# Down products with side jobs: the next half's first low half tied behind the first addition, and the jobs behind the additions written so far

## The chip, the cores and the metric

The kernel runs on one core of a Trainium2 chip. The metric is the device time of one execution in microseconds (us), as the median of several runs. The engines are named as in the profile: PE is the tensor engine's matmuls and PEld its weight loads, DVE the vector engine, ACT the scalar engine, POOL the GpSimd engine, SP the engine whose queue issues most loads. L524 is line 524 of the kernel before.

## What is computed

A trunk of four layers over 512 positions of width 1024, in float32. Each layer has a mixer (two S5 layers, one gated linear attention, one differential attention) and then a feed-forward product:

```python
def swiglu_ffn(h, w_gate_up, w_down):
    g, u = jnp.split(h @ w_gate_up, 2, axis=-1)
    return (jax.nn.silu(g) * u) @ w_down
...
    for layer in range(DEPTH):
        kind = layer % N_MIXERS
        ...
        x = x + mix.astype(x.dtype)
        h = rmsnorm(x, norm_ffn[layer])
        x = x + swiglu_ffn(h, ffn_w_gate_up[layer], ffn_w_down[layer]).astype(x.dtype)
```

`w_gate_up` is 1024 by 5632 and `w_down` 2816 by 1024. The change lies in the down product, `(...) @ w_down`, of layers 0 and 1.

## The kernel before

**Products in three matmuls.** Each float32 operand is split into a high half in the format that PE multiplies quickly and a low half, the rest. A product of two 128-wide tiles is three matmuls, high by high, high by low and low by high (`mm3`, L396 to L398). A block of weights, 256 rows by 512 columns, goes through four steps: a load of 512 KB into a staging buffer (`staged`, tile `wst`, 3 buffers), a cast on ACT that makes the high half (`high`, L368, tile `whl`, 5 buffers), a subtraction on DVE that makes the low half (`low`, L376), and 24 matmuls (2 k-tiles by 4 row tiles by 3). A staging buffer is free again when its low half is made.

**The feed-forward stage.** `ffn` works through the hidden width in groups of blocks of 256: groups of 3, 3, 3 and 2 blocks in layer 0, and of 4, 4 and 3 in the others. For each group it makes the gate and up products (`seven_block`, seven block products each, L541), which leaves the activations in `act`, and then calls `gemm_b` twice, once for each 512 columns of the output (d = 0 and d = 1, the two halves), which multiplies the group's activations by its rows of `w_down`. A half accumulates in four PSUM banks, one for each 128 positions (t = 0 to 3). In the last k-tile each finished bank is added into x on DVE, scaled by a column r (L524, in `add_x`), which also frees the bank: the next half's products for tile t need it. In the last group each addition is followed by the next layer's norm for that tile (`left.take`: a multiplication on DVE, L107, then transposes on PE and a split of the result). The last group's second half has a tail: its last four k-tiles run tile by tile instead (in layer 0, where the last group has four k-tiles, that is the whole half).

**Side jobs.** Layers 0 and 1 use their down products to prepare operands for later mixers. A generator (`s5_spilled` in layer 0; `diff_tables` and then `s5_phases_spilled` in layer 1) is stepped once behind each tile's three matmuls (`self.job()`), and each step writes a few small instructions: on DVE (L1129 to L1131 and L1246 in layer 0, L1306 to L1312 in layer 1), on ACT, small matmuls on PE, and DMAs in POOL's queue. In layer 0 a round of the generator has 17 steps, with work in steps 1, 3, 5, 7, 9, 11 and 13 to 16, eight rounds in all; in layer 1 it is 13 steps of tables and then eight rounds of 14, of which the first eight do work.

**Order.** Within these stages the order of each engine's instructions is not written by hand. A planner that runs when the kernel is built keeps a modelled clock, and gives each engine the earliest-written instruction that is ready on it; the engines then run their queues in that order. `issue_after(ins)` adds an edge of order alone: what its block writes on the engine of `ins` is queued behind `ins`, with no wait. `job` uses it with every entry of `self.last`, the latest instruction of each of several kinds (high, low, scaled, silu, mm and others). `gemm_b` with jobs writes the split of the next weight block ahead of the current block's matmuls (`nxt`). In a first half, the later blocks' splits are tied behind the last gate's `silu` and `scaled` (`behind`).

Of the kernel before, what the change touches and what calls it, by code (L numbers as in the profile page):

```python
# [16 lines left out]
ALU = mybir.AluOpType  # L17
# [22 lines left out]
class Slices:  # L40


    def __init__(self, *tiles):
        self.ts, self.known = [[self.flat(t), 0] for t in tiles], {}
# [116 lines left out]
class Sides(Left):  # L161
# [27 lines left out]
    def ahead(self, n):  # L189

        w = [self.tr.staged(self.quarter(0, 0, b), 4, 256) for b in range(len(self.heads), len(self.heads) + n)]
        self.heads += [self.tr.halves(y, 4, 256) for y in w]
# [96 lines left out]
class Trunk:  # L289
    def __init__(self, ctx, tc, ins, out):  # L290
        self.ctx, self.tc, self.nc = ctx, tc, tc.nc
        self.i = ins
        self.out = out
        self.rot = self.edges = 0
        nc = self.nc
        ep = lambda name, bufs, **k: ctx.enter_context(tc.tile_pool(name=name, bufs=bufs, **k))
        self.cp = ep("const", 1)
        self.xp = ep("xp", 1)
        self.hp = ep("hp", 2)
        self.wp = ep("wp", 3)  # L300
        self.np_ = ep("normp", 2)
        self.sp = ep("small", 8)
        self.ps = ep("psum", 1, space=PSUM)
        self.dp = ep("dram", 1, space=DRAM)
        self.ident = self.cp.tile([P, P], F32, name="ident")
        make_identity(nc, self.ident)
        self.two_pi = float(np.nextafter(np.float32(TWO_PI), np.float32(0)))
        self.mhalf = self.cp.tile([P, 8], F32, name="mhalf")
        nc.vector.memset(self.mhalf[:], -0.5)
        self.ones = self.cp.tile([P, P], F32, name="ones")  # L310
        nc.gpsimd.memset(self.ones[:], 1.0)
        self.dq = nc.sync
        self.jobs = iter(())
        self.last = {}
        self.pend = []
        self.guard, self.lazy = None, False
        self.behind = None

    def edge(self, pool, n):

# [79 lines left out]
    def gemm_b(self, stat, w, nk, c0, evac, k0=0, tail=0, between=(), ahead=None, jobs=False, behind=None):  # L400

        between = iter(between)
        accs = [self.acc() for _ in range(NT)]
        hl = nxt = None
        for kb in range(0, nk - tail, 2):
            hl = nxt or self.wb(w, k0 + kb, c0)
            self.behind = behind
            nxt = self.wb(w, k0 + kb + 2, c0) if jobs and kb + 2 < nk - tail else None  # L410
            if kb == 2:
                self.flush()
            for a in range(2):
                k = kb + a
                for t in range(NT):
                    self.mm3(
                        accs[t][:], stat(k, 0, t), stat(k, 1, t), hl[:, 0, a], hl[:, 1, a],
                        k == 0, k == nk - 1,
                    )
                    if k == nk - 1:  # L420
                        evac(t, accs[t])
                    if jobs:
                        self.job()
            next(between, lambda: None)()
        self.behind = None
        if tail:
            hls = [self.wb(w, k0 + kb, c0) for kb in range(nk - tail, nk, 2)]
            if ahead:
                self.hand_all()
                ahead()  # L430
            for t in range(NT):
                for j in range(tail):
                    k = nk - tail + j
                    self.mm3(
                        accs[t][:], stat(k, 0, t), stat(k, 1, t), hls[j // 2][:, 0, j % 2],
                        hls[j // 2][:, 1, j % 2], k == 0, k == nk - 1,
                    )
                evac(t, accs[t])
# [76 lines left out]
    def add_x(self, d, left=None, r=None):  # L515

        nc = self.nc

        def evac(t, ps):
            xs = self.x[:, t, d * 512 : (d + 1) * 512]  # L520
            if r is None:
                nc.vector.tensor_tensor(xs, xs, ps[:], op=ALU.add)
            else:
                nc.vector.scalar_tensor_tensor(xs, ps[:], r[:, t : t + 1], xs, op0=ALU.mult, op1=ALU.add)  # L524
            if left is not None:
                left.take(t, d)

        return evac
# [2035 lines left out]
```

## Time and profile before

| what | value |
|---|---|
| time, median of 3 runs | 2266.39 us (2264.08 to 2268.05) |
| time of the profiled execution | 2265.08 us |
| span of the profiled execution | 2263.3 us |
| PE busy | 2200.7 us, 97% of the span |
| PEld busy | 1952.7 us, 86% |
| DVE busy | 1561.8 us, 69% |
| ACT busy | 1121.4 us, 50% |
| POOL busy | 281.2 us, 12% |
| additions into x, L524 | 96, median 0.75 us each |
| low halves, L376 | median 1.22 us each |

How to read it: a row of a timeline has the start and the duration in us, the engine, the line, the operation, the tiles written and read, the shape and the count, and in brackets how long the engine was idle before it and what it waited for. Instructions on DVE overlap a little: the next starts up to 0.09 us before the recorded end. The profiled execution's sums are made against its own 2265.08 us.

### The profile page before, as it was taken

The page shows a single profiled execution, that of the slowest core. Times are in us where ns is not written, and L with a number is a line of the kernel's source. Part 1 is how long each engine was busy: PE and PEld are TensorE (multiplying, and loading weights), DVE is VectorE, ACT ScalarE, POOL GpSimd, SP SyncE. Part 2 cuts the span into 40 slices and gives each one's busy share as a digit, 9 for nine tenths or more (in the row PEclk, how much of TensorE's full clock was granted, in tenths as well). Part 3 has the DMA queues.
Part 4 walks back from the last instruction along what each step waited for, and adds up shares of the span by engine and source line. Part 5 has one row for each costly group of instructions (what it writes and reads, how often), then busy time and mean ns, then how long its engine had stood idle before and what let it go on. Part 6 is the DMA issues. An engine that isn't in the chain of part 4 may idle for free.

```text
span 2263.3 us, 37243 instructions
## 1 busy us (share of the span) xinstructions
PE 2200.7 (97%) x14847; PEld 1952.7 (86%) x14847; DVE 1561.8 (69%) x2424; ACT 1121.4 (50%) x1878; POOL 281.2 (12%) x392
## 2 busy tenths in 40 slices
PE   5999999999999999999999999999999899999998
PEld 4878979889777799998988887999998788989997
DVE  9963977776625479777754675977766964967675
ACT  6534645453453456555535676744544224635343
POOL 1000141522000011101002131111000100101000
PEclk8999999999999999999999999999999999999999
DMA  4257475663422557766336366985641546676632
GB/s 88 52 154 188 115 192 159 172 188 90 124 75 65 142 143 185 191 162 172 99 127 142 91 147 161 237 219 134 175 101 39 147 144 166 169 186 158 168 75 75
DMA packets 296039, 317.83 MB, mean 140 GB/s; under 512 B 72285, under 2 KB 235417, under 8 KB 295482
## 3 DMA queue, kind: packets, MB, share of 16 engines
q1 hardware_dynamic: 233626, 234.23, 34.4%
q0 software_dynamic: 62240, 81.22, 19.3%
q8 instruction: 117, 1.92, 0.4%
q14 instruction: 56, 0.46, 0.1%
HBM read 283.54 MB, written 16.65 MB: 133 GB/s over the span
## 4 chain that ended last, share of the span: by engine, by line
PE 83%; DVE 8%; ACT 4%; issue 2%; DMA 1%; SPq 1%; POOL 0%; ACTq 0%; DVEq 0%; POOLq 0%
PE a L541 18%; PE acc L396 14%; PE acc L398 13%; PE acc L397 13%; PE c L541 8%; PE d L541 4%; PE y L1504 2%; DVE whl L376 2%; ACT whl L368 1%; PE V L1468 1%; PE op L2366 1%; PE s L2332 1%; PE tp L123 1%; DVE halves L229 1%; ACT halves L211 1%
## 5 line engine op out<-in xcount | busy, mean ns | idle before, releaser
L376 DVE TENSOR_TENSOR whl<-wst,whl 128x1024 fp32r<-128x1024 f32 x272 | 331.2, 1222 | 260.7 <-ACT whl L368 260.2
L368 ACT CAST whl<-wst 128x1024 fp32r<-128x1024 f32 x272 | 283.9, 1050 | 310.3 <-PE acc L398 227.2
L541 PE MATMUL a<-side,whl 128*128 128x256 f32 x3168 | 382.3, 277 | 4.0 <-DVE whl L376 3.6
L541 PEld LDWEIGHTS a<-side,whl 128*128 128x128 f32 x3168 | 369.0, 188 | 6.8 <-DVE whl L376 5.4
L396 PE MATMUL acc<-whl,act 128*128 128x512 f32 x680 | 268.9, 396 | 1.9 <-DVE x L524 1.9
L397 PE MATMUL acc<-whl,act 128*128 128x512 f32 x680 | 265.3, 390 | 0.0
L398 PE MATMUL acc<-whl,act 128*128 128x512 f32 x680 | 265.3, 390 | 0.0
L541 PE MATMUL c<-side,whl 128*128 128x256 f32 x2112 | 254.3, 277 | 1.2 <-DVE whl L376 1.2
L541 PEld LDWEIGHTS c<-side,whl 128*128 128x128 f32 x2112 | 246.7, 188 | 2.0 <-DVE whl L376 2.0
L376 DVE TENSOR_TENSOR whl<-slot,whl 128x1024 fp32r<-128x1024 f32 x107 | 130.4, 1221 | 70.4 <-ACT whl L368 70.4
L396 PEld LDWEIGHTS acc<-whl,act 128*128 128x128 f32 x680 | 127.6, 188 | 31.3 <-issue 2.7
L368 ACT CAST whl<-slot 128x1024 fp32r<-128x1024 f32 x107 | 112.2, 1053 | 83.0 <-PE acc L398 34.9
L398 PEld LDWEIGHTS acc<-whl,act 128*128 128x128 f32 x680 | 127.7, 188 | 27.0
L397 PEld LDWEIGHTS acc<-whl,act 128*128 128x128 f32 x680 | 127.7, 188 | 24.7
L396 PE MATMUL acc<-whl,hT 128*128 128x512 f32 x352 | 142.6, 405 | 0.0
L398 PE MATMUL acc<-whl,hT 128*128 128x512 f32 x352 | 138.1, 392 | 0.0
L397 PE MATMUL acc<-whl,hT 128*128 128x512 f32 x352 | 137.8, 392 | 0.0
L541 PE MATMUL a<-sides,whl 128*128 128x256 f32 x1056 | 134.5, 283 | 0.0
L541 PEld LDWEIGHTS a<-sides,whl 128*128 128x128 f32 x1056 | 129.7, 191 | 1.2
L541 PE MATMUL d<-sides,whl 128*128 128x256 f32 x1056 | 126.5, 276 | 1.0 <-ACT whl L368 1.0
L541 PEld LDWEIGHTS d<-sides,whl 128*128 128x128 f32 x1056 | 122.8, 188 | 1.2 <-ACT whl L368 1.2
L680 ACT CAST act<-r 128x512 fp32r<-128x512 f32 (+1 forms) x110 | 66.4, 646 | 114.9 <-DVE r L659 107.6
(478 smaller groups left out, 3909.9 us busy)
## 6 DMA issues: line engine op xcount, KB each, us to landing
wst<-in_ffn_w_gate_up_dram SPq DMA_DIRECT2D x88, 512.0 KB, 4.7
wst<-in_ffn_w_down_dram SPq DMA_DIRECT2D x88, 512.0 KB, 4.4
slot<-in_ffn_w_gate_up_dram SPq DMA_DIRECT2D x71, 512.0 KB, 5.3
wst<-in_ffn_w_gate_up_dram POOLq DMA_DIRECT2D x44, 512.0 KB, 6.3
halves<-in_ffn_w_gate_up_dram SPq DMA_DIRECT2D x43, 512.0 KB, 5.4
wst<-in_s_w_glu_dram SPq DMA_DIRECT2D x32, 512.0 KB, 4.7
wst<-in_gla_w_in_dram SPq DMA_DIRECT2D x24, 512.0 KB, 3.7
wst<-in_diff_w_qkv_dram SPq DMA_DIRECT2D x24, 512.0 KB, 4.4
```

The source lines that it names most:

```text
L123: tr.nc.tensor.transpose(p[:, j], h[:, j * P : (j + 1) * P], tr.ident[:])
L211: self.tr.nc.scalar.mul(self.F[t // 2, d][:, j, (t % 2) * P : (t % 2 + 1) * P], p[:, j], self.gcol[:, 4 * d + j : 4 * d + j + 1])
L229: v.tensor_tensor(s, s, y, op=op)
L368: self.last["high"] = self.nc.scalar.copy(hl[:, 0], w[:])
L376: self.last["low"] = self.nc.vector.tensor_tensor(hl[:, 1], w[:], hl[:, 0].bitcast(F32), op=ALU.subtract)
L396: mm(out, lh, rh, start=first, stop=False)
L397: mm(out, lh, rl, start=False, stop=False)
L398: self.last["mm"] = mm(out, ll, rh, start=False, stop=last)
L541: mm(o, hl[:, x, k, c], side[y][:, k], start=first and not (j or k or n), stop=k == 3 and n == 2, skip_group_check=True,)
L680: self.last["act high"] = nc.scalar.copy(dst[:, 0, j], src[:, j])
L1468: mm(V[kk][z][:, bs(b)], inm[:, z, bs(b)], U[:, bs(b)], start=True, stop=True)
L1504: mm(yb[:, b], q[:, j, b], om[:, j // 2, bs(b)], start=False, stop=j == 3)
```

## The change

`gemm_b`, when it has side jobs and an addition of the previous half is known, now writes the split of its first weight block itself, ahead of the loop: load, high half, and the low half with an edge behind `self.added`, the addition of tile 0 of the half before. The block is then used as the loop's first. `add_x` records each scaled addition in `self.last["x"]`, so that every later step of the side jobs is queued behind it on DVE, and the one of tile 0 in `self.added`. After the test `self.added` is set to None.

```diff
-        self.behind = None
+        self.behind = self.added = None
...
         hl = nxt = None
+        if jobs and self.added is not None:
+            src = self.staged(self.wb_src(w, k0, c0), 2, 512)
+            nxt = self.high(src, 2, 512)
+            with self.tc.issue_after(self.added.ins):
+                self.low(nxt, src)
+        self.added = None
         for kb in range(0, nk - tail, 2):
             hl = nxt or self.wb(w, k0 + kb, c0)
...
-                nc.vector.scalar_tensor_tensor(xs, ps[:], r[:, t : t + 1], xs, op0=ALU.mult, op1=ALU.add)
+                self.last["x"] = nc.vector.scalar_tensor_tensor(
+                    xs, ps[:], r[:, t : t + 1], xs, op0=ALU.mult, op1=ALU.add
+                )
+                if t == 0:
+                    self.added = self.last["x"]
```

The test also holds for a first half (the addition known there is that of the group before, long issued) and for the last group of layer 0, whose second half has no loop.

## The prediction

> **What bounds the kernel now.** I read the page first, then a table of stretches around the down products of layers 0 and 1 (the only ones with side jobs), then the timelines of VectorE (DVE) and TensorE (PE) at each change of half. Three of the stretches: width, then busy time of PE, PEld, DVE, ACT and POOL, granted clock, DMA share and GB/s.
>
> ```profile
> 286.00:330.00 44.00, 43.16 (x311) 32.26 (x310) 35.65 (x82) 20.98 (x49) 26.13 (x41) 1.00 0.74 189
> 386.00:430.00 44.00, 44.00 (x321) 33.84 (x320) 36.26 (x82) 21.38 (x50) 26.94 (x46) 1.00 0.57 153
> ...
> 1006.00:1057.00 51.00, 49.90 (x248) 42.06 (x247) 37.03 (x68) 27.69 (x43) 7.96 (x11) 1.00 0.67 178
> ```
> PE is busy without a break in the second; in the first it lacks 0.84 us and in the last 1.10 us. The kernel is bound by PE, so only PE's idle time can be won, and DVE (36 to 37 of 44 to 51 us) matters only where PE waits for it.
>
> I call the changes from the first 512 columns to the second: a1, a2, a3 (layer 0, groups one to three), a4 (its last group, where the second half has a tail alone), b1, b2, b3 (layer 1). The clean picture of one is in layer 2, which has no side jobs:
>
> ```profile
> 1520.06 2.79 DVE L524 SCALAR_TENSOR_TENSOR x<-acc,rturned,x 128x512 f32<-128x512 f32 x4 [1.09 <-PE acc L398]
> ...
> 1521.90 0.39 PE L396 MATMUL acc<-whl,act 128*128 128x512 f32 x1
> 1522.13 0.39 PE L397 MATMUL acc<-whl,act 128*128 128x512 f32 x1
> ```
> DVE waits for PE, then adds the four tiles into x, 2.79 us in all; the second half's first matmul starts 1.84 us behind the start of the first addition, and matmuls follow each other at 0.23 us. Call the natural start of the first addition E. The second half's first matmul of tile 0 runs at E+1.84 and needs that addition and the weights' high half; the next, at E+2.07, needs the low half. Now a1 and b2, DVE rows first, then PE's wait:
>
> ```profile
> 306.43 1.22 DVE L376 TENSOR_TENSOR whl<-wst,whl 128x1024 fp32r<-128x1024 f32 x1 [2.69 <-ACT whl L368]
> 307.57 0.74 DVE L524 SCALAR_TENSOR_TENSOR x<-acc,rcol,x 128x512 f32<-128x512 f32 x1
> 308.23 0.35 DVE L1131 TENSOR_TENSOR halves<-halves 128x192 f32<-128x192 f32 x1
> 308.49 1.40 DVE L524 SCALAR_TENSOR_TENSOR x<-acc,rcol,x 128x512 f32<-128x512 f32 x2
> 309.81 0.41 DVE L1129 TENSOR_TENSOR halves<-halves,pw 128x256 f32<-128x256 f32 x1
> 310.14 0.42 DVE L1130 TENSOR_TENSOR halves<-halves,pw 128x256 f32<-128x256 f32 x1
> ...
> 308.37 0.50 PE L396 MATMUL acc<-whl,act 128*128 128x512 f32 x1 [0.84 <-DVE x L524]
> ```
>
> ```profile
> 1031.34 0.60 DVE L1310 SCALAR_TENSOR_TENSOR spare<-mrow,s5flo,spare 128x128 f32<-128x128 f32 x2
> 1031.87 1.21 DVE L376 TENSOR_TENSOR whl<-wst,whl 128x1024 fp32r<-128x1024 f32 x1
> 1033.01 2.71 DVE L524 SCALAR_TENSOR_TENSOR x<-acc,rcol,x 128x512 f32<-128x512 f32 x4
> ...
> 1033.89 0.47 PE L396 MATMUL acc<-whl,act 128*128 128x512 f32 x1 [1.10 <-DVE x L524]
> ```
> In both a subtraction for a low half (L376, 1.22 us) stands ahead of the first addition, and PE waits for the addition: 0.84 and 1.10 us. It is not the next half's first low half, though. Counting weight blocks of 24 matmuls against L376, the row at 306.43 belongs to the next group's first gate product, that at 1031.87 to the second half's fourth block. The first low half ran far earlier, as b1 shows:
>
> ```profile
> 902.30 0.42 DVE L1306 TENSOR_SCALAR cssp<-cssp 128x512 f32<-128x512 f32 x1
> ...
> 904.44 0.34 DVE L1309 SCALAR_TENSOR_TENSOR spare<-mrow,s5fhi,cssp 128x128 f32<-128x128 f32 x1
> 904.70 1.22 DVE L376 TENSOR_TENSOR whl<-wst,whl 128x1024 fp32r<-128x1024 f32 x1
> ...
> 910.63 2.71 DVE L524 SCALAR_TENSOR_TENSOR x<-acc,rcol,x 128x512 f32<-128x512 f32 x4
> ```
> Here it is the row at 904.70, nearly 8 us ahead of its use (the additions at 910.63 and the 1.84 above put that at 912.4), with side jobs (L1306, L1309) on both sides.
>
> **The change part by part.** (1) The low half of the second half's first block may not be issued before the first addition. An addition holds DVE 0.66 us (307.57 to 308.23) and the subtraction takes 1.22: placed right behind the first addition it ends at E+1.88, ahead of the need at E+2.07; placed later, PE stands. (2) DVE's side jobs may not overtake the latest addition written before them. (3) Where the low half waits, its staging buffer does too: there are three, so the load of the fourth block (b1, b2) or of the next gate block (layer 0) starts only then, and its low half can no longer stand ahead of the first addition. That block is wanted two blocks of 24 x 0.23 = 5.5 us later at the earliest, against 4.4 us from issue to landing:
>
> ```profile
> wst<-in_ffn_w_down_dram SPq DMA_DIRECT2D x88, 512.0 KB, 4.4
> ```
> So the later load costs nothing (without that cover PE would wait a few us), and the two stalls go: -0.84 and -1.10.
>
> So the question is where DVE's queue puts the low half. The planner takes for each engine the earliest-written instruction that is ready on its own clock. In the rows of b1 the low half gives way to L1306 and L1309, which are written before it, though they are side jobs; when an operation's successor isn't ready yet, the next one in the text goes. In the changed kernel the low half is written behind all four additions and behind the side jobs of the half's last four steps, and those side jobs can no longer have been run early: each is tied to its addition. What they are, by counting the generators' steps (24 steps a half in layer 0, 32 in layer 1; 17 a round in layer 0, 13 and then 14 a round in layer 1):
>
> a1, steps 20 to 23: three operations of L1129 to L1131 at the first tile, three larger ones at the third. From the rows above a small operation holds DVE 0.26 us (308.23 to the next start), a large one 0.33 (309.81 to 310.14). Ahead of the low half: 4 x 0.66 + 3 x 0.26 + 3 x 0.33 = 4.4, end at E+5.6; without the large ones, if they aren't ready, E+4.7. PE needs it at E+2.07 and can fill 3 x 0.23 = 0.7 with the other tiles' first matmuls. Loss 1.9 to 2.9; I take 2.5, and the 0.84 of now goes: +1.7. Were the low half right behind the addition: 0 loss, -0.84.
>
> b1, steps 28 to 31: L1306 and three pairs L1309, L1310. Ahead of the low half stand four additions (2.64), L1306 (0.34, from 902.30 to the next start) and about five of the 0.27 us pieces (1.35): it ends at E+5.5. Loss 5.5 - 2.07 - 0.7 = 2.7, nothing now: +2.7, at the least 0.
>
> b2, steps 92 to 95: empty steps. Only additions compete: the low half goes second (no loss) or fifth (2.64 + 1.22 = E+3.9, loss 1.1). The second addition becomes ready 0.68 behind the first, which holds DVE 0.66, so the profile can't say; I take the middle, 0.6: -0.5 with the 1.10 removed.
>
> a2: an empty step, then nine tiny operations, but PE runs side matmuls between the tiles, which leaves DVE a hole: 0 to 2, I take 0.4. a3: no DVE jobs of size at the first tiles, and a hole: 0.
>
> b3 has no jobs left, but the next layer's norm follows each addition:
>
> ```profile
> 1127.86 1.43 DVE L524 SCALAR_TENSOR_TENSOR x<-acc,rcol,x 128x512 f32<-128x512 f32 x2 [0.25 <-PE acc L398]
> 1129.20 1.28 DVE L107 TENSOR_TENSOR hh<-x,gain 128x512 f32<-128x512 f32 x2
> ```
> L107 holds DVE 0.6 for each tile and is written ahead of the low half, as are the transposed tiles' own subtractions. In second place the low half crowds the rest by at most 0.5. Last, behind four additions and four L107 (2.64 + 2.4), it ends at E+6.3; PE has 0.7 of first matmuls and about 0.6 of transposes to do meanwhile, so the loss is 2.9. I take 0.9, nearer to the hole: the next addition isn't ready before E+0.68, L107 not before its addition has ended.
>
> a4: the guard asks only for jobs and an addition, not for a main loop. With a tail of 4 of 4 k-tiles the loop is empty, so a fourth block is loaded, cast and subtracted for nothing, and the tail loads its own two. That is one DMA of 512 KB, a cast on ACT (busy 21 of 44 us in the first stretch, so at no cost), 1.22 us on DVE, and a staging buffer held until the first addition. SP's queue now, and the first product that follows:
>
> ```profile
> 568.90 0.37 SPq L1958 DMA_DIRECT2D wal<-in_gla_w_in_dram  x1
> 570.64 17.41 SPq L357 DMA_DIRECT2D wst<-in_gla_w_in_dram  x4
> ...
> 590.47 0.48 PE L396 MATMUL any<-hT,whl 128*128 128x512 f32 x1
> ```
> The next mixer's first load, which would get the held buffer, is issued at 568.90, the wide ones from 570.64, and the product at 590.47: a delay of 8 us there has cover. Less has the tail's second block, whose load moves back by one buffer into the time of the additions: 0 to 3 us (a landing of 4.4 less the 1.4 of PE's work on the first block); I take 0.5, because PE can do the other tiles' share of the first block meanwhile (4 x 6 x 0.23 = 5.4 us).
>
> The side jobs themselves come later, at b1 by some 8 us (L1306 from 902.30 to behind the first addition), and with them their DMAs in POOL's queue and their small matmuls on PE. The generators end 24 and 35 steps of 0.7 us ahead of the last half, and I cost this at nothing; without that cover the matmuls among them would make PE wait.
>
> Sum: 1.7 + 2.7 - 0.5 + 0.4 + 0 + 0.9 + 0.5 = +5.7 us. The profiled execution took 2265.08 us; 2265.08 + 5.7 = 2270.8. It lies 1.3 under the median of the runs shown, 2266.39, so the median comes to 2272.1. With every term at its best the sum is -0.84 - 1.10 = -1.9, with every one at its worst 2.9 + 2.7 + 1.1 + 2 + 2.9 + 3 - 1.9 = +12.7.
>
> **A rule on the clock.** Idle PE can cost more than its own time. Where PE last waited long (busy 0.46 of 2 us), the granted clock is 1.00, and then 0.59 and 0.50 for two stretches; behind the 1.10 us of b2 it is 1.00:
>
> ```profile
> 1766.00:1768.00 2.00, 0.46 (x2) 0.30 (x2) 2.00 (x2) 0.00 (x0) 0.00 (x0) 1.00 0.63 141
> 1768.00:1770.00 2.00, 1.12 (x4) 1.00 (x4) 2.00 (x5) 0.00 (x0) 0.00 (x0) 0.59 0.94 238
> 1770.00:1772.00 2.00, 2.00 (x10) 1.83 (x9) 2.00 (x5) 0.00 (x0) 0.00 (x0) 0.50 0.93 344
> ...
> 1032.60:1035.60 3.00, 1.90 (x9) 1.45 (x9) 3.00 (x5) 2.59 (x5) 0.42 (x1) 1.00 0.78 262
> ```
> The four us from 1768 lost 2 x 0.41 + 2 x 0.50 = 1.8 us of PE's work, behind 1.5 us of idleness. The 2.5 us at a1 and 2.7 at b1 could bring the same, 1.8 us each. [...]
>
> **The rivals.**
> Low half in time: at a1, b1 and b2 the planner finds DVE free of ready jobs and sets the low half second. Then the two stalls go and little comes: -1.9 + 0.5 for the spare block = -1.4, 2265.0. For it: b2 has no jobs, and side jobs often lack data (DVE idles 2.69 us ahead of 306.43); against: the jobs tied to the first tile at a1 and b1 are of a round whose inputs are there. It decides if the low half ends before E+2.07. This is the side without a loss. It would have to find 4.5 us, and PE lacks only 1.94 in these stretches, to be measurably faster.
> Clock: the stalls come and lower the clock twice: 5.7 + 2 x 1.8 = 9.3, 2275.7. For it the rows above; against it that PE does single matmuls within the stall.
> Nothing moves at the halves (the two stalls stay, since other ready low halves take the freed place), and the spare block alone costs 0 to 1: 2267.
>
> **How the numbers follow.** Low half late: 0.45, at 2272.1. Its own range has a1 at 1.9, b2, a2 and a4 at nothing and b3 at 0.5, +3.2 or 2269.6, up to b3 at 2.9 and a4 at 2, +9.2 or 2275.6. As 0.2% (4.5 us) is about what a measurement of this kernel can tell from no change, a quarter of this case counts as no difference. In time: 0.32. Clock: 0.10. Nothing moves: 0.10. Left over, mostly a new order in the stages behind that loses or wins some us: 0.03. Slower: 0.34 + 0.10 + 0.02 = 0.46; within 0.2%: 0.11 + 0.32 + 0.07 = 0.50; faster: 0.04. The range goes from just under the best sum (2266.4 - 1.9 = 2264.5) to the late case's upper end with one fall of the clock, 2275.6 + 1.8: 2264.0 to 2277.5.
>
> **What would show it.** In the changed kernel's timeline, the first addition at a1 and b2 starts about 1.84 us ahead of the second half's first matmul (right step 3). L376 for that half follows behind all four L524 at a1 and b1, and PE shows the first matmuls of several tiles in a run and then a wait for DVE whl of 2 to 3 us (right main term); a low half between the first and the second addition, and no PE wait there, shows the rival. One more L368 and L376 and one more 512 KB load in layer 0 show the spare block. It is wrong if PE's waits for whl in these stretches sum to less than 1 us, or if the granted clock falls there.

## The result, and the profile after

| kernel | median | lowest to highest |
|---|---|---|
| before, beside it | 2266.57 us (6 runs) | 2264.08 to 2270.36 |
| changed | 2286.99 us (6 runs) | 2284.74 to 2291.05 |

The change makes the kernel 0.9% slower: the ratio is 1.0089, 95% interval 1.0079 to 1.0098, 20.4 us. Forecast were 2272.1 us and a range of 2264.0 to 2277.5. The sign of the likeliest case was right, the size was not.

In the rows below lines behind the edit have moved: L524 is now L530, L541 is L551, L1129 to L1131 are L1139 to L1141, L1306 to L1310 are L1316 to L1320 and L495 is L501; L376 and L396 to L398 are where they were. From the page of the changed kernel, the span, the busy times, three groups (count, busy time and mean ns, then idle time ahead and what ended it) and the weight loads:

```profile
span 2289.3 us, 37232 instructions
...
PE 2218.1 (97%) x14847; PEld 1960.9 (86%) x14847; DVE 1564.1 (68%) x2425; ACT 1124.7 (49%) x1879; POOL 281.6 (12%) x392
...
L376 DVE TENSOR_TENSOR whl<-wst,whl 128x1024 fp32r<-128x1024 f32 x273 | 332.9, 1223 | 280.7 <-ACT whl L368 280.2
...
L396 PE MATMUL acc<-whl,act 128*128 128x512 f32 x680 | 270.7, 399 | 5.2 <-DVE x L530 5.0
L397 PE MATMUL acc<-whl,act 128*128 128x512 f32 x680 | 270.3, 398 | 3.9 <-DVE whl L376 3.9
...
wst<-in_ffn_w_down_dram SPq DMA_DIRECT2D x89, 512.0 KB, 4.0
```
Two things stand there. L397, the first matmul that needs a low half, now waits 3.9 us for L376, and L396 waits 5.0 us for the additions (1.9 before). And PE is busy 17.4 us longer (2218.1 against 2200.7) with the same matmuls. Their records are longer for two reasons: the clock fell (below), and a matmul that has waited alone is recorded at 0.5 us where one in a row takes 0.39. The 89th load is the spare block.

The first change of half, a1, in the timeline: VectorE's rows, then TensorE's:

```profile
307.99 1.23 DVE L376 TENSOR_TENSOR whl<-wst,whl 128x1024 fp32r<-128x1024 f32 x1 [1.97 <-ACT whl L368]
309.13 0.74 DVE L530 SCALAR_TENSOR_TENSOR x<-acc,rcol,x 128x512 f32<-128x512 f32 x1
...
310.33 0.74 DVE L530 SCALAR_TENSOR_TENSOR x<-acc,rcol,x 128x512 f32<-128x512 f32 x1
...
312.58 0.74 DVE L530 SCALAR_TENSOR_TENSOR x<-acc,rcol,x 128x512 f32<-128x512 f32 x1
313.25 0.42 DVE L1141 TENSOR_TENSOR halves<-halves 128x256 f32<-128x256 f32 x1
313.58 1.22 DVE L376 TENSOR_TENSOR whl<-wst,whl 128x1024 fp32r<-128x1024 f32 x1
...
309.93 0.51 PE L396 MATMUL acc<-whl,act 128*128 128x512 f32 x1 [0.40 <-DVE x L530]
311.12 0.49 PE L396 MATMUL acc<-whl,act 128*128 128x512 f32 x1 [0.69 <-DVE x L530]
312.05 0.50 PE L396 MATMUL acc<-whl,act 128*128 128x512 f32 x1 [0.43 <-DVE x L530]
313.38 0.79 PE L396 MATMUL acc<-whl,act 128*128 128x512 f32 x1 [0.83 <-DVE x L530]
314.85 0.79 PE L397 MATMUL acc<-whl,act 128*128 128x512 f32 x1 [0.67 <-DVE whl L376]
315.44 0.63 PE L398 MATMUL acc<-whl,act 128*128 128x512 f32 x1
315.87 0.63 PE L397 MATMUL acc<-whl,act 128*128 128x512 f32 x1
```
The low half is the row at 313.58, behind four additions and six side jobs, 4.45 us behind the first addition. Until then PE can do four matmuls, each behind a wait for its tile's addition (0.40 to 0.83 us). And once the low half is there, the matmuls start 0.43 us apart instead of 0.23: the clock is at half (granted 0.50 from 313.0 to 319.9 us). Stretches of the changed kernel, with the columns of the prediction's table; the granted clock is the third figure from the right:

```profile
307.00:315.00 8.00, 4.98 (x17) 2.73 (x15) 7.01 (x13) 2.88 (x6) 6.73 (x12) 0.88 0.62 160
315.00:321.00 6.00, 6.00 (x30) 4.43 (x31) 4.07 (x10) 0.74 (x2) 1.27 (x2) 0.60 0.98 232
416.00:420.00 4.00, 1.91 (x8) 1.03 (x7) 4.00 (x12) 1.52 (x4) 4.00 (x8) 1.00 0.41 124
...
928.00:934.00 6.00, 5.85 (x14) 4.59 (x15) 5.22 (x16) 1.99 (x3) 1.50 (x3) 0.50 0.88 156
1048.00:1054.00 6.00, 4.96 (x18) 2.95 (x17) 5.30 (x8) 3.37 (x6) 0.00 (x0) 0.98 0.61 199
1054.00:1060.00 6.00, 6.00 (x21) 4.79 (x22) 6.00 (x20) 2.00 (x3) 2.43 (x3) 0.74 0.91 178
```
The clock falls behind a1, b1, b2 and b3 (there for 3.4 us from 1156.1), not behind a2 (416). In the kernel before there is no half-clock row at any of them.

The time by place. A stage reaches from the end of the gate product ahead of a down product to the first gate matmul behind it. Loss is the stage's growth in the profiled runs, clock is half the length of the half-clock stretch in it, and the rest is called waiting (it holds the longer records of single matmuls too):

| place | loss, us | half clock for | clock, us | waiting, us | forecast (no clock) |
|---|---|---|---|---|---|
| a1 | 5.55 | 6.8 | 3.4 | 2.1 | +1.7 |
| a2 | 2.69 | 0 | 0 | 2.7 | +0.4 |
| a3 | 0.01 | 0 | 0 | 0.0 | 0 |
| a4, to layer 1 | 1.25 | as before | 0 | 1.25 | +0.5 |
| b1 | 6.40 | 6.8 | 3.4 | 3.0 | +2.7 |
| b2 | 2.59 | 3.4 | 1.7 | 0.9 | -0.5 |
| b3, to layer 2 | 5.39 | 3.4 | 1.7 | 3.7 | +0.9 |
| sum | 23.9 | | 10.2 | 13.7 | +5.7 |

With 2.0 us ahead of layer 0's first gate product, where nothing was changed, this is the 26.0 by which the span grew. The profiled run is the slowest of the six. Over all six, the mean granted clock is 0.9897, which makes (1 - 0.9897) x 2286 = 23.6 us of clock lost; in 18 and 27 runs of the kernel before it is 15.1 and 16.0. So of the 20.4 us between the medians about 8 are clock and about 12 are waiting. The mean also counts the half-clock stretch at the kernel's start, 17.1 us in the profile before and 13.7 us in this one, so the split is known to 1 or 2 us only.

### The profile page after: what moved, and what is told of

Same layout as the page of the kernel before. It is cut to its first block, busy times and chain, and to the rows that moved or that the text cites. A ratio compares the mean times of both kernels' runs of the same rounds, so it can differ in the third digit from the quotient of the medians.

```text
span 2289.3 us, 37232 instructions
## 1 busy us (share of the span) xinstructions
PE 2218.1 (97%) x14847; PEld 1960.9 (86%) x14847; DVE 1564.1 (68%) x2425; ACT 1124.7 (49%) x1879; POOL 281.6 (12%) x392
## 4 chain that ended last, share of the span: by engine, by line
PE 79%; DVE 11%; ACT 4%; issue 3%; DMA 2%; SPq 1%; POOL 0%; DVEq 0%; ACTq 0%; POOLq 0%
PE a L551 17%; PE acc L398 12%; PE acc L397 12%; PE acc L396 12%; PE c L551 8%; PE d L551 4%; DVE whl L376 3%; PE y L1514 2%; ACT whl L368 2%; PE op L2376 1%; PE s L2342 1%; PE V L1478 1%; DMA wst<-in_ffn_w_down_dram 1%; PE tp L123 1%; DVE halves L229 1%
## 5 line engine op out<-in xcount | busy, mean ns | idle before, releaser
L376 DVE TENSOR_TENSOR whl<-wst,whl 128x1024 fp32r<-128x1024 f32 x273 | 332.9, 1223 | 280.7 <-ACT whl L368 280.2
L551 PE MATMUL a<-side,whl 128*128 128x256 f32 x3168 | 382.6, 277 | 4.1 <-DVE whl L376 3.6
L551 PEld LDWEIGHTS a<-side,whl 128*128 128x128 f32 x3168 | 369.4, 188 | 6.8 <-DVE whl L376 5.3
L396 PE MATMUL acc<-whl,act 128*128 128x512 f32 x680 | 270.7, 399 | 5.2 <-DVE x L530 5.0
L397 PE MATMUL acc<-whl,act 128*128 128x512 f32 x680 | 270.3, 398 | 3.9 <-DVE whl L376 3.9
L398 PE MATMUL acc<-whl,act 128*128 128x512 f32 x680 | 268.8, 395 | 0.0
L551 PE MATMUL c<-side,whl 128*128 128x256 f32 x2112 | 254.2, 277 | 1.2 <-DVE whl L376 1.2
L551 PEld LDWEIGHTS c<-side,whl 128*128 128x128 f32 x2112 | 246.6, 188 | 2.0 <-DVE whl L376 2.0
L376 DVE TENSOR_TENSOR whl<-slot,whl 128x1024 fp32r<-128x1024 f32 x107 | 130.5, 1223 | 72.5 <-ACT whl L368 72.5
L396 PEld LDWEIGHTS acc<-whl,act 128*128 128x128 f32 x680 | 128.4, 189 | 38.8 <-DVE x L530 9.9
L397 PEld LDWEIGHTS acc<-whl,act 128*128 128x128 f32 x680 | 130.0, 191 | 31.4 <-DVE whl L376 5.7
L398 PEld LDWEIGHTS acc<-whl,act 128*128 128x128 f32 x680 | 130.1, 191 | 27.4
L396 PE MATMUL acc<-whl,hT 128*128 128x512 f32 x352 | 142.5, 405 | 0.0
L398 PE MATMUL acc<-whl,hT 128*128 128x512 f32 x352 | 138.0, 392 | 0.0
L397 PE MATMUL acc<-whl,hT 128*128 128x512 f32 x352 | 138.0, 392 | 0.0
L551 PE MATMUL a<-sides,whl 128*128 128x256 f32 x1056 | 134.3, 283 | 0.0
L551 PEld LDWEIGHTS a<-sides,whl 128*128 128x128 f32 x1056 | 129.7, 191 | 1.0
L551 PE MATMUL d<-sides,whl 128*128 128x256 f32 x1056 | 126.6, 276 | 1.0 <-ACT whl L368 1.0
L551 PEld LDWEIGHTS d<-sides,whl 128*128 128x128 f32 x1056 | 122.9, 188 | 1.2 <-ACT whl L368 1.2
```

What stands on the lines that cost most here:

```text
L376: self.last["low"] = self.nc.vector.tensor_tensor(hl[:, 1], w[:], hl[:, 0].bitcast(F32), op=ALU.subtract)
L396: mm(out, lh, rh, start=first, stop=False)
L397: mm(out, lh, rl, start=False, stop=False)
L398: self.last["mm"] = mm(out, ll, rh, start=False, stop=last)
L551: mm(o, hl[:, x, k, c], side[y][:, k], start=first and not (j or k or n), stop=k == 3 and n == 2, skip_group_check=True,)
```

## The experiments

Theories. L: the low half's place in VectorE's queue makes the waits. J: the side jobs, tied behind the additions, crowd them and make the waits. S: the spare block costs. C: the waits lower the clock, and that is a large part of the loss; W is its opposite.

**The low half's tie alone, and the side jobs' tie alone.** In the first, the additions are no longer entered in `self.last`:

```diff
-                self.last["x"] = nc.vector.scalar_tensor_tensor(
+                x = nc.vector.scalar_tensor_tensor(
...
-                    self.added = self.last["x"]
+                    self.added = x
```


> The low half of the next half's first block stays tied behind the first addition (and stays in the order after all four), the tie of the side jobs to the additions is taken out. Theory L (the low half's late place makes most of the loss): most of the 20.4 us stay, 2279 to 2286 us, and at the first change of layer 0 and of layer 1 the first L397 still waits for the low half. Theory J (side jobs between the additions make it): the additions close up, 2267 to 2272 us. Theory C (the clock's fall after a wait gives half of the loss, wherever the wait is from) goes with either: where a wait over 2 us in all stays, a stretch at 0.5 of the clock follows it, 3.4 or 6.8 us long, and without such waits the half-clock rows of the kernel before are all there is.

In the second, the early block goes instead:

```diff
-        if jobs and self.added is not None:
-            src = self.staged(self.wb_src(w, k0, c0), 2, 512)
-            nxt = self.high(src, 2, 512)
-            with self.tc.issue_after(self.added.ins):
-                self.low(nxt, src)
```


> The side jobs stay tied behind the additions; the early block of the next half, its tie and the spare block are taken out, so that its low half stands ahead of the four additions again. Theory L: no L397 waits for a low half, so near the kernel before, 2265 to 2270 us, with single waits of the L396 for the additions of under 1 us each. Theory J: the additions of the first change of layer 0 still stand 1.3 to 2 us apart, the four L396 still wait 2.4 us in all, and with the clock's fall behind it the time is 2274 to 2284 us.

Measured: the low half's tie alone 2285.49 us (4 runs), ratio 1.0085 (1.0071 to 1.0099). The side jobs' tie alone 2267.85 (11 runs), ratio 1.0001 (0.9992 to 1.0010). PE's waits over the down products of layers 0 and 1 (240 to 1170 us: in total, times, longest), in the kernel before, the changed one, the first and the second:

```profile
PE acc L396 <- DVE x L524: 1.9, 2, 1.1
```
```profile
PE acc L396 <- DVE x L530: 5.0, 12, 0.8
PE acc L397 <- DVE whl L376: 3.9, 4, 1.4
```
```profile
PE acc L397 <- DVE whl L376: 3.2, 5, 1.0
PE acc L396 <- DVE x L530: 2.2, 8, 0.8
```
```profile
PE acc L396 <- DVE x L525: 0.9, 2, 0.7
```
Theory L holds, and J falls as the main cause. With the side jobs tied and the low half early, no matmul waits for a low half, and although side jobs still stand between the additions at a1, PE waits 0.9 us there in all. The reason is the order PE has to follow: where the low half is early, PE has three matmuls to do for each addition; where it is late it has one, and the same spacing of the additions becomes four waits.

By place the first differs from the changed kernel more than in sum. At b1 no side job stands between its additions: PE waits 0.16 and 0.63 us, no half-clock stretch follows, and the stage loses 1.66 us (6.40 in the changed kernel). At b2 it loses 4.69 us (2.59), with a wait of 1.20 us for a cast and 6.8 us at half clock. So the jobs' tie costs nothing by itself, but beside a late low half it lengthens the waits at b1. Theory C fits both: in the first, half clock follows waits of 2.1 us (a1), 1.7 (b2) and 2.3 (b3) in sum and none of 1.1 (a2) and 0.8 (b1); in the second there is none at any change.

**The spare block left out.**

```diff
-        if jobs and self.added is not None:
+        if jobs and self.added is not None and nk > tail:
```


> As changed, but the spare block of layer 0's last group (a 512 KB load, a cast and a low half whose result nobody reads) is left out. Theory S (the spare block costs, since it takes a weight buffer and 1.1 us each of two engines in the densest group): 1 to 4 us less than the changed kernel, 2283 to 2286 us, all of it between the start of the last down group of layer 0 and the start of layer 1. Theories L, J and C: that stretch lost 1.25 us in the profiled run, so 2285.5 to 2287 us.

Measured: 2287.88 us (4 runs), ratio 1.0100 (1.0085 to 1.0115), no better than the changed kernel. In the stretch itself the profile shows the 0.6 us wait gone that the changed kernel has at its first product after a4, and with the half-clock stretch at 655 to 668 us set off (6.8 us here, 3.4 there) the stage is about 1.5 us shorter. That much is the spare block's price by one profile each; the times can't show it.

This run tells something else. Its waits at b2 are those of the changed kernel and those at b3 nearly so (2.1 us in sum, 1.8 there), but the clock did not fall. The waiting rows of its timeline at b2,

```profile
1048.95 0.50 PE L396 MATMUL acc<-whl,act 128*128 128x512 f32 x1 [0.16 <-DVE x L530]
1049.61 0.50 PE L396 MATMUL acc<-whl,act 128*128 128x512 f32 x1 [0.16 <-DVE x L530]
1050.73 0.50 PE L397 MATMUL acc<-whl,act 128*128 128x512 f32 x1 [0.63 <-DVE whl L376]
```
and its stretch behind b2, at full clock:

```profile
1052.00:1058.00 6.00, 6.00 (x28) 4.98 (x27) 5.91 (x17) 2.93 (x4) 1.61 (x3) 1.00 1.02 225
```
b2 lost 0.69 us here and 2.59 there, b3 3.98 and 5.39. The differences, 1.9 and 1.4, are about half of the 3.4 us stretches (1.7): nearly the same waits, with and without the clock's fall.

**The low half put first.** One added context makes the planner take the low half right behind the first addition:

```diff
-            with self.tc.issue_after(self.added.ins):
+            with self.tc.issue_after(self.added.ins), self.tc.high_priority():
```


> As changed, but the low half of the early block is put first among what DVE may do once the first addition is issued, so that it stands between the first and the second addition at all seven changes, where it stood behind all four additions at a1, a2, b2, b3 and in the middle at a3. Nothing else is taken out: the side jobs stay behind the additions, the spare block stays. Theory L: 2264 to 2271 us; no wait for the low half over 0.5 us is left, the second addition comes 1.1 us later and its tile waits that long at most. Theory J: the second to fourth additions are now later still, by 1.1 us, and the four L396 wait 3 us or more: 2284 to 2292 us. Theory C: the half-clock rows behind a1, b1, b2 and b3 go exactly where the sum of the waits falls under about 2 us.

Measured: 2272.39 us (8 runs), ratio 1.0027 (1.0017 to 1.0037), 1.4 us over the upper end of theory L's forecast and far from J's. a1 in this kernel:

```profile
306.84 0.75 DVE L530 SCALAR_TENSOR_TENSOR x<-acc,rcol,x 128x512 f32<-128x512 f32 x1
307.50 1.22 DVE L376 TENSOR_TENSOR whl<-wst,whl 128x1024 fp32r<-128x1024 f32 x1
...
309.17 0.75 DVE L530 SCALAR_TENSOR_TENSOR x<-acc,rcol,x 128x512 f32<-128x512 f32 x1
...
307.64 0.50 PE L396 MATMUL acc<-whl,act 128*128 128x512 f32 x1 [0.26 <-DVE x L530]
308.77 0.50 PE L397 MATMUL acc<-whl,act 128*128 128x512 f32 x1 [0.63 <-DVE whl L376]
```
The stage is 0.08 us longer than before, 5.5 shorter than in the changed kernel, although the second addition starts 2.33 us behind the first, where it was 1.20. No half-clock stretch is left at any of the seven changes. So 14.6 of the 20.4 us, the clock's part included, hang on one instruction's place in DVE's queue at each change. What is not won: the low half ends 0.6 us too late for PE even in second place.

**Matmuls to fill the waits.** 42 matmuls whose result nobody reads, at five changes:

```diff
+        early = nxt is not None and c0 > 0 and nk > tail
...
+                    if early and k == 0:
+                        opened.append(self.opened)
...
+            if early and kb == 0:
+                fill = self.sbank("fill") if FILL[self.nfill] else None
+                for t, n in enumerate(FILL[self.nfill]):
+                    with self.tc.issue_after(opened[t].ins):
+                        for i in range(n):
+                            self.nc.tensor.matmul(
+                                fill[:], stat(0, 0, t), hl[:, 0, 0], start=True, stop=True,
+                            )
+                self.nfill += 1
```


> The changed kernel with 42 more matmuls whose result nobody reads, into a bank of their own, 128x512 of 0.227 us each, issued behind the first matmuls of the next half at a1, a2, b1, b2 and b3, in the gaps in which these matmuls wait; additions, side jobs and the late low half stay in the order of the changed kernel. They are 9.5 us of work and the waits there were about 12 us, so they should lengthen nothing by more than 1 or 2 us. Theory C (the clock halves because the waits leave TensorE idle, and that is 10 of the 20 us): no half-clock stretch behind a1, b1, b2 and b3 is left, and the time is 2277 to 2281 us although the kernel does more. Theory W (the loss is all waiting, the half-clock stretches come by chance or cost nothing beside it): 2286 to 2290 us.

Measured: 2284.23 us (5 runs), ratio 1.0071 (1.0058 to 1.0084). Behind a1, b1, b2 and b3:

```profile
313.00:319.00 6.00, 5.72 (x52) 4.20 (x52) 4.72 (x12) 0.91 (x3) 1.09 (x2) 1.00 1.01 229
...
925.00:931.00 6.00, 5.53 (x24) 3.96 (x23) 6.00 (x17) 1.90 (x3) 1.89 (x2) 1.00 0.43 74
...
1050.00:1056.00 6.00, 6.00 (x29) 4.96 (x27) 6.00 (x20) 2.67 (x4) 2.27 (x3) 1.00 0.85 170
...
1151.00:1157.00 6.00, 5.59 (x26) 4.48 (x27) 3.30 (x4) 0.73 (x3) 0.00 (x0) 1.00 0.49 154
```
The half-clock stretches are gone at all four, as C says, with additions and low half as late as before (at a1 the low half starts 4.44 us behind the first addition, 4.45 in the changed kernel), and the mean granted clock over the runs is back at 0.9932, 15.5 us lost, as in the kernel before. a1's stage lost 3.02 us instead of 5.55, b1's 3.62 instead of 6.40. So it is idleness that lowers the clock here, and more work in the same time keeps it up: PE was busy for 7.07 of the 8.00 us from 305 at a clock of 1.00, in the changed kernel for 4.98 of the 8.00 from 307 at 0.88. The time missed C's forecast by 3 us: I had taken the four stretches of one profile for the usual run (10 us; over the runs it is 8), the filled stages lost 1.7 us more than the changed kernel's without its clock, and a4's stage lost 3.65 us instead of 1.25, 1.7 of it by a half-clock stretch at 663 us, which the kernel before has at 655.6 and the changed one at 668.0, for 3.4 us each.

**The low half's place alone, without b3, and free.** The first has the context above, no tie of the side jobs and only changes of half (`c0 > 0 and nk > tail`). The second leaves b3 out as well (`c0 > 0 and not tail`). The third is the first without the tie, so that the low half runs when its cast is done.

> Only the low half's place is left of the change, and only where the half of a group changes (a1, a2, a3, b1, b2, b3): it is put between the first and the second addition. The tie of the side jobs and the spare blocks are out. Theory L: no matmul waits for a low half, the waits of the kernel before at a1 (0.84 us) and b2 (1.10 us) go, b3 keeps the 1.75 us that the kernel with the low half first lost there: 2265 to 2269 us. Theory J predicts a gain against the kernel with the low half first (2272.4 us), of 3 us or more, for the jobs' tie taken out alone; theory L less than 3 us.

> As the one with the low half's place alone, but b3 (the last group of layer 1) is left as in the kernel before. If b3 lost its 1.75 us because the low half there pushes three additions back that the next layer's casts also wait for: 2264.5 to 2267 us, at best 1.9 us under the kernel before. If the loss at b3 came from elsewhere: no different from the one before it.

> The early block with its low half first in rank but tied to nothing, so that it runs as soon as its cast is done, some microseconds ahead of the first addition; jobs not tied, no spare blocks. Theory L: the low half is never waited for, and the additions are no later than in the kernel before: 2264.5 to 2268 us. If the early block itself (its load and cast one block sooner) costs, it shows here with nothing else changed: over 2268 us.

Measured, 11 runs each: 2270.52 us, ratio 1.0015 (1.0006 to 1.0024); 2269.24, 1.0009 (1.0000 to 1.0018); 2271.72, 1.0022 (1.0013 to 1.0030). None is faster than the kernel before, and all three lie above what I expected. The third lies where I had put it if the early block itself costs (over 2268 us); its profile, of its slowest run (2276.70), doesn't settle that. b3's stage lost 0.90 us in the first's profile and won 0.36 where b3 was left out. The gain on the low half put first with everything else left in is 1.9 us, under the 3 that J asked for. b2 in the second shows the old wait, which the first two keep (the third waits 1.7 us there instead, put down to a side job on ACT):

```profile
1032.38 1.22 DVE L376 TENSOR_TENSOR whl<-wst,whl 128x1024 fp32r<-128x1024 f32 x1
1033.52 0.74 DVE L530 SCALAR_TENSOR_TENSOR x<-acc,rcol,x 128x512 f32<-128x512 f32 x1
1034.18 1.21 DVE L376 TENSOR_TENSOR whl<-wst,whl 128x1024 fp32r<-128x1024 f32 x1
...
1034.41 0.47 PE L396 MATMUL acc<-whl,act 128*128 128x512 f32 x1 [0.82 <-DVE x L530]
1035.45 0.50 PE L397 MATMUL acc<-whl,act 128*128 128x512 f32 x1 [0.57 <-DVE whl L376]
```
Another block's low half still stands ahead of the first addition (0.82 us of wait, where it was 1.10), and the tied one adds 0.57. The side jobs' tie would have moved that low half forward (see step (3) below): with the tie, in the kernel with the low half first, b2's stage is 0.75 us shorter than before, without it 0.71 and 0.59 us longer. In the third a1 won 0.90 us, but a2 lost 2.99 in that profile; the first and the second, which are alike at a2, lost 1.41 and 0.10 there. What makes the rest of these differences of 1 to 3 us between kernels and runs is left open.

**The other low halves behind the first addition.** The kernel before, with the tie on the blocks that really stood ahead of the additions:

```diff
+            if jobs and c0 > 0 and kb == 2:
+                self.late = self.added
...
+            with self.tc.issue_after(self.late.ins) if self.late is not None else nullcontext():
+                self.low_now(hl, w)
```


> The kernel before, with another tie: not the low half of the next half's first block, but the low halves written after it (the later blocks of the second half and of the next group's gate products) may not be issued before the first addition of the first half; layers 0 and 1 only. In the kernel before, one of these stands right ahead of the first addition at a1 and b2, and PE waits 0.84 and 1.10 us there. If these rows are the whole cause of the two waits, both go and nothing takes their place: 1.9 us less, 2264 to 2266 us. If the place of any low half near the additions only moves the wait: 2266 to 2268 us.

Measured: 2266.23 us (11 runs), ratio 1.0000 (0.9991 to 1.0009). b2 won 0.74 us; at a1 nothing is won, because three side jobs moved into the place that the low half left, and the first matmul waits 1.2 us there. The wait moved, as the second forecast said.

**A ladder of waits.** In layers 2 and 3, where there are no side jobs, the low half behind the fourth addition, made once to four times over:

```diff
+        if not jobs and self.fourth is not None and c0 > 0 and not tail:
+            src = self.staged(self.wb_src(w, k0, c0), 2, 512)
+            nxt = self.high(src, 2, 512)
+            with self.tc.issue_after(self.fourth.ins):
+                for _ in range(1 + self.rungs.pop(0)):
+                    self.low_now(nxt, src)
```


> The kernel before, with the low half of the second half's first block tied behind the fourth addition at the four changes of layers 2 and 3 that have no tail (no side jobs there), and written once, twice, three and four times over in that order (the repeats write the same values again), so that the waits of PE grow in steps of one subtraction, 1.14 us. By the sum of the prediction: the low half ends at E+3.9 (4 x 0.66 + 1.22), 2.07 and the 0.7 us of the other tiles' first matmuls off, so 1.1, 2.3, 3.4 and 4.5 us of waiting, 11.3 in all: 2277 to 2279 us without the clock. Theory C: half-clock stretches follow the longer of them, and the stage then loses half of the stretch more: 2279 to 2288 us. [...]

> The same with the four lengths in the other order, four, three, two and one subtraction, so that a length is seen in another place: the same waits and times for the same lengths, 2277 to 2288 us in all. If the half-clock stretches follow the place and not the length, they stay where they were in the other ladder.

Measured: 2289.18 us (4 runs), ratio 1.0105 (1.0090 to 1.0120), and 2287.13 (4 runs), 1.0096 (1.0082 to 1.0109): 1.2 us over theory C's range, and just inside it. From the timeline, the first matmul that needs the low half (L399 there, the low half is L378), at two rungs of the ladder up and at the first of the ladder down:

```profile
1524.07 0.50 PE L399 MATMUL acc<-whl,act 128*128 128x512 f32 x1 [0.63 <-DVE whl L378]
...
1648.07 0.61 PE L399 MATMUL acc<-whl,act 128*128 128x512 f32 x1 [2.90 <-DVE whl L378]
```
```profile
1528.16 0.79 PE L399 MATMUL acc<-whl,act 128*128 128x512 f32 x1 [5.42 <-DVE whl L378]
```

| wait, us | ladder up: stage loss, half clock | ladder down: stage loss, half clock |
|---|---|---|
| 0.63 | 1.91, none | 1.36, none |
| 2.90 | 5.26, 3.4 | 6.19, 6.8 |
| 4.16 | 7.39, 6.8 | 6.68, 3.4 |
| 5.42 | 8.93, 6.8 | 8.18, 6.8 |

In both ladders half clock follows the waits of 2.90 us and more, in whichever place they lie, and not the one of 0.63. The first step is larger than one subtraction (2.3 us), since another block's low half went between the repeats.

## Why the prediction was wrong

**The place was right, and its price without the clock nearly.** The question was "where DVE's queue puts the low half", and at a1 and b1 it stands where the prediction had it, behind all four additions and the side jobs (at a1 it ends 5.7 us behind the start of the first addition, for E+5.6). Without the clock a1 and b1 came to 2.1 and 3.0 us, for +1.7 and +2.7. The waits look different, though. The prediction's sign was several first matmuls in a run and then one wait of 2 to 3 us for the low half; in the rows above each first matmul waits for its own addition, and L397 only 0.67 us. And what the prediction named as a sign of being wrong, a fall of the granted clock there, came.

**The step that failed first: the middle between two orders.** At b2, a2 and b3 the prediction had both ends, second or last, and took a middle or leaned to the early one because of a hole between two additions. In the changed kernel the low half was last at all three (fifth in the queue at b2, behind four additions and ten side jobs at a2, behind the additions, four L107 and two transposed tiles' subtractions at b3):

```profile
416.64 0.75 DVE L530 SCALAR_TENSOR_TENSOR x<-acc,rcol,x 128x512 f32<-128x512 f32 x1
...
418.11 1.22 DVE L376 TENSOR_TENSOR whl<-wst,whl 128x1024 fp32r<-128x1024 f32 x1
...
1156.07 1.22 DVE L376 TENSOR_TENSOR whl<-wst,whl 128x1024 fp32r<-128x1024 f32 x1
```
These three terms stood at +0.8 together and came to 7.3, 6.5 of the 8 us by which the waiting was too small. A middle between the two orders fits neither: the low half went last among what was ready. Only at a3, where the next addition was not ready and DVE had that hole, did it go second, between the first addition (514.70) and the second (516.50), and cost nothing, as forecast:

```profile
515.37 1.22 DVE L376 TENSOR_TENSOR whl<-wst,whl 128x1024 fp32r<-128x1024 f32 x1
```
The prediction's worst sum, +12.7, was nearer to the 13.7 than the taken one; at b3 it counted the transposes as work that PE has meanwhile, and they waited 0.70 and 0.63 us for DVE themselves.

**The step that failed second: the clock.** It was a rival at 0.10 with two falls of 1.8 us. The runs show it as about 8 us, up to four falls of 1.7 or 3.4 us. The sum puts no term for the clock behind its waits of up to 2.7 us, an estimate that no run shows: in the changed kernel the clock fell behind a1, b1, b2 and b3 and not behind a2. The argument against it, "that PE does single matmuls within the stall", was wrong: at a1 PE was busy for 1.50 of the 3.41 us ahead of the fall. The rows of 1766 to 1772 had shown a fall behind a short wait; the prediction quoted them and still gave them one chance in ten, and it priced a fall by the four us shown there, where the stretch at half clock lasts 6.8 us (1768.3 to 1775.2).

**Step (3) failed at both its places, a1 and b2, and b2's -1.10 came by another step.** The staging buffers did not hold the other low half back. At a1 it still stands ahead of the first addition (307.99 above), so the first L396 waits 0.40 us on top. At b2 the load of the fourth block (the last ahead of the gate blocks' loads) goes out 10 us before the tied low half starts (1052.48), as soon as another low half (1041.29 to 1042.51) has given up its buffer. The fourth block's low half is again the row right ahead of the additions:

```profile
1042.54 0.37 SPq L357 DMA_DIRECT2D wst<-in_ffn_w_down_dram  x1
...
1048.70 1.23 DVE L376 TENSOR_TENSOR whl<-wst,whl 128x1024 fp32r<-128x1024 f32 x1 [3.41 <-ACT whl L368]
1049.84 2.72 DVE L530 SCALAR_TENSOR_TENSOR x<-acc,rcol,x 128x512 f32<-128x512 f32 x4
```
The first matmul starts 0.89 us behind the first addition (1050.73), not the 1.84 that step (3) was to show, and yet no wait is recorded ahead of it. DVE was idle until that low half's cast was done; in the kernel before, side jobs (L1309 and L1310) held it up. It is the jobs' tie, step (2), that took them away: with that tie alone, and no early block, b2 has no wait either and its stage is 1.36 us shorter.

```profile
1030.51 1.23 DVE L376 TENSOR_TENSOR whl<-wst,whl 128x1024 fp32r<-128x1024 f32 x1 [2.94 <-ACT whl L368]
```
So that term of the sum was right by luck. The experiment that held such low halves back saw three side jobs take the place at a1.

**Side jobs later, at no cost:** right for the tie alone, 0.6 us, inside its interval; beside the late low half it lengthened b1's waits. **Spare block:** 0.5 forecast, 1.25 to 1.5 in the profiles. **Low half in time** (0.32, 2265.0): where it was put in second place the kernel took 2269 to 2272 us. The end at E+1.88 was counted from a first addition that starts at E. At a1 of the kernel with the low half first, the first matmul could have run at 307.38 (307.64 less its wait), which puts E at 305.54; the addition started at 306.84, behind another block's low half, and so the tied one ended 1.3 us later than the sum had it. It was step (3) that failed here too.

## What to carry to other kernels

An edge of order does not say "right behind", it says "not ahead of": whoever is written late and tied late comes behind all that is ready, and what waits for it is to be costed for the last place, unless the trace shows a hole ahead of it. Here, the waits at a1, b1, b2 and b3 of the changed kernel brought half clock behind them, for 6.8, 6.8, 3.4 and 3.4 us, which cost 1.7 or 3.4 us more each; those at a2, and those at b2 and b3 in the run without the spare block, brought none. So a forecast with several waits of 2 to 3 us has to count both. If the tied instruction is urgent, give it a rank as well as an edge.

## What the runs showed of the hardware

In the changed kernel's profile the granted clock is 0.50 from 313.0 us on for 6.8 us (a1), from 927.4 for 6.8 (b1), from 1053.7 for 3.4 (b2) and from 1156.1 for 3.4 (b3). The distances between these starts are 180, 37 and 30 times 3.413 us, the lengths two, two, one and one times. The other half-clock stretches of this profile and all of the one before lie on such a grid too, counted from 2.4 us behind the span's start in this profile and from 0.2 us in the other; apart from the last, which the kernel's end cuts off, they are 3.4, 6.8, 13.7 and 17.1 us long.

PE's busy time in the 3.41 us ahead of a fall, and in as many us at three places without one:

| place, profile | from, us | PE busy, us of 3.41 | share | granted clock behind |
|---|---|---|---|---|
| a1, changed | 309.62 | 1.50 | 0.44 | 0.50 for 6.8 us |
| b1, changed | 924.02 | 1.70 | 0.50 | 0.50 for 6.8 us |
| b2, changed | 1050.31 | 2.40 | 0.70 | 0.50 for 3.4 us |
| b3, changed | 1152.71 | 2.08 | 0.61 | 0.50 for 3.4 us |
| a2, changed | 415.43 | 1.86 | 0.54 | 1.00 |
| b2, before | 1031.07 | 2.31 | 0.68 | 1.00 |
| start of layer 3, before | 1754.70 | 1.54 | 0.45 | 1.00 |
| the same | 1758.11 | 1.59 | 0.47 | 0.50 for 3.4 us |
| the same | 1764.94 | 1.51 | 0.44 | 0.50 for 6.8 us |
| layer 1's mixer, before | 652.19 | 3.41 | 1.00 | 0.50 for 3.4 us |

So at a1 the clock fell although PE had a matmul running for 0.44 of the time ahead. The share alone does not tell where it falls: 0.45 and 0.54 are without a fall, 0.61 and 0.70 with one. The stretch from 655.6 us, from 668.0 in the changed kernel, begins behind 3.41 us in which matmuls ran all the time; its cause is open. The two profiles that differ at b2 and b3 had PE busy about as much: for 4.96 of 6.00 us (from 1048) and 7.00 of 9.00 (from 1149) in the changed kernel, with a fall, and for 5.05 of 6.00 (from 1046) and 6.73 of 9.00 (from 1144) in the run without the spare block, without one. What decides there is open.
